# An mLSTM output gate computed with features on the partitions and multiplied in behind the transposition

## The chip, the cores and the metric

The kernel runs on one core of a Trainium2 chip (eight cores on two dies). The metric is the device time of one execution in microseconds (us); lower is better. A core has a matrix engine (TensorE, PE in the profile, PEld its weight loads), a vector engine (VectorE, DVE), a scalar engine (ScalarE, ACT), GpSimd (POOL) and a queue engine (SyncE, SP) that here only issues DMAs. Each engine takes its instructions in the order in which they were built. ScalarE issues DMAs too, in that same order.

## The reference, cut to what matters

One layer of a diffusion backbone over 1024 latent tokens and 256 context tokens, width 1024, in 32-bit floats. Two token mixers, windowed attention and a bidirectional mLSTM, are merged and followed by a ConvFFN. The change is in the end of the mLSTM. With `h_tilde` its output for 4 heads of 256 features:

```python
def mlstm_readout(h_tilde, o_pre, norm_w):
    B, L = h_tilde.shape[:2]
    hn = rms_norm(h_tilde, norm_w.reshape(ML_HEADS, ML_V_DIM)).reshape(B, L, ML_V_W)
    return hn.astype(o_pre.dtype) * jax.nn.sigmoid(o_pre)
```

`o_pre` is a projection of the normed input (1024 tokens x 1024 features to 1024 x 256 per head): the output gate. So each head's output is normed over its 256 features, multiplied by a weight per feature, and by the sigmoid of the gate, element by element. The result then goes through a projection, for which it has to lie with features on the partitions.

## The kernel before, in words

Everything is one program for one core. The stages follow each other: start-up, attention, mLSTM (`stage_mlstm`, L682 to L1086), merge and output projection (`stage_tail`, from L1089), ConvFFN. Every product of two 32-bit matrices is made of three matmuls (`mm3`, L86, lines L91 to L93): each operand is split into a high and a low part (`split_from`, L47: the high part on ScalarE at L44, the low part on VectorE or GpSimd at L49), and high x high, low x high and high x low are added up in PSUM.

The normed input lies transposed in SBUF as `hT`: eight pairs of tiles of 128 features x 1024 tokens. The mLSTM goes through four heads. The loop at L1072 records for each head: `core` (the recurrence over ten chunks in both directions), `decays` of the next head, `proj_o` (the gate), `readout`, then for the next head `proj_kv` and `states`, then `turn` of this head, then `proj_q` and `trans_k` of the next head and three or four `branch_sums`. The order in which the instructions stand on each engine is not that of the recording: a planner of the recording layer sets it, engine by engine, by expected durations and the recorded order as priority, so that matmuls of `proj_o` are laid between those of `core`. What it sets is fixed in the program.

What the steps do, with their lines:

- `core` (L951): `S` = q.k (L961), weighted with the decays on VectorE (`ub`, L965), split into `sh` and `sl`; per chunk and direction two products into PSUM, `o` (L976) and `i` (L978); the numerator `nm` from `i` on ScalarE (L980) and `o` on VectorE (L981); a few short instructions for the denominator (L983 to L985); the output `hf` (L987 on GpSimd or L989 on VectorE). The state: `kwh` on GpSimd (L929), `kwl` on VectorE (L930), the product `dC`, the update `C` on VectorE (L937), and its split into `CH` (ScalarE) and `CL` (VectorE), which the next chunk's `i` reads. `decays` adds masks (`ub`, L910 on GpSimd) and takes exponentials on ScalarE (L912).
- `proj_o` (L766): per head 8 products of 128 tokens x 256 gate features. `hT` is stationary (128 features x 128 tokens), the weights `w1h`, `w1l` move (256 columns): 24 matmuls a product, 192 a head. ScalarE copies each out of PSUM (L774) into `sg`, two tiles for the two halves of 512 tokens; for the last head with the sigmoid.
- `readout` (L1007): the sigmoid over a whole half on ScalarE (L1011, not for the last head), squares and sums of `hf` on ScalarE (`rj`, L1015), the reciprocal root on GpSimd (`rr`, L1016, L1017), and one VectorE instruction per 128 tokens (L1020): `hf` x `rr` x `sg`.
- `turn` (L1022): per half and per 128 features four TensorE transposes (L1028) into a PSUM tile `mt`, one ScalarE copy with the norm weight as scale per partition (L1030) into `mo`, and a store to DRAM on SP (L1031). `mo` has two buffers, shared with the scratch tile of the squares.
- `branch_sums` (L1038): sums and differences of weight and attention tiles for the merge, which have nothing to do with the heads. One round takes both tiles with the tag `sg` (two buffers in all), loads four pieces with DMAs that ScalarE issues (L1046, L1054), makes four VectorE subtractions or additions (L1047 to L1050, L1055 to L1058), and stores four results with DMAs on SP (L1061). Its names are `s_ba`, `t_at`, `s_bm`. Two rounds are recorded within `proj_kv` of the first head, three, four and three behind the `trans_k` of heads 1, 2 and 3.
- `proj_kv` (L723), `proj_q` (L743), `trans_k` (L755): keys, values and queries of a head; the products of `proj_q` have the weights stationary and 512 tokens of `hT` moving, into `q`. PSUM tiles: two for `mm` (kv, q, S, mo), three for `tp` (o, i, transposes).
- In the tail, the first operands of the merge (`baah`, `baal`, `bawh`, `bawl`, products `yb`) are recorded to be issued behind the last instruction of the last readout (`E.turned`, L1020, used at L1228).

The functions that the diff touches and what calls them:

Of the kernel before, what the change touches and what calls it, by code (L numbers as in the profile page):

```python
# [8 lines left out]
F32 = mybir.dt.float32  # L9
F32R = mybir.dt.float32r  # L10
AF = mybir.ActivationFunctionType
ALU = mybir.AluOpType
# [4 lines left out]
P = 128  # L17
# [5 lines left out]
NB = L // P  # L23
# [5 lines left out]
MLH = 4  # L29
DQK = 128  # L30
DV = 256
# [54 lines left out]
def mm3(nc, ps, lhs, rhs, ls, rs, start=True, stop=True):  # L86
    n = len(lhs)
    for i in range(n):
        lh, ll = lhs[i]
        rh, rl = rhs[i]  # L90
        nc.tensor.matmul(ps, lh[:, ls], rh[:, rs], start=start and i == 0, stop=False)  # L91
        nc.tensor.matmul(ps, lh[:, ls], rl[:, rs], start=False, stop=False)  # L92
        nc.tensor.matmul(ps, ll[:, ls], rh[:, rs], start=False, stop=stop and i == n - 1)  # L93


def sl(a, n):
    return slice(a, a + n)
# [3 lines left out]
def layer_kernel(ctx: ExitStack, tc: tile.TileContext, A: dict, out: bass.AP, dbg=None):  # L101
# [76 lines left out]
    with ExitStack() as st:  # L178
        stage_mlstm(E, st)
# [502 lines left out]
def stage_mlstm(E, st):  # L682
    nc, tc, A, ident, expo, hT, wts, dr = E.nc, E.tc, E.A, E.ident, E.expo, E.hT, E.wts, E.dr
    mm_tile, tp_tile, s_tile, mlT_d, gtile = E.mm_tile, E.tp_tile, E.s_tile, E.mlT_d, E.gtile
# [8 lines left out]
    mlw = mp.tile([P, 2 * MLH], F32, name="mlw")  # L693
# [14 lines left out]
    H = {}  # L708
# [46 lines left out]
    def trans_k(h):  # L755
# [7 lines left out]
            kT.append((kh, kl))  # L763
        H[h]["kT"] = kT

    def proj_o(h):  # L766
        w = H[h]["wqo"]
        sgs = [rp.tile([P, 4, DV], F32, tag="sg", name=f"sg{h}_{t}", bufs=2) for t in range(2)]
        for cc in range(NB) if h % 2 else range(NB - 1, -1, -1):
            ps = mm_tile(f"mo{h}_{cc}")  # L770
            mm3(nc, ps[:, :DV], hT, w, sl(cc * P, P), sl(DQK, DV))

            fn = AF.Sigmoid if h == MLH - 1 else AF.Copy
            nc.scalar.activation(sgs[cc // 4][:, cc % 4], ps[:, :DV], fn)  # L774
        H[h]["sg"] = sgs

    GC = {}
# [223 lines left out]
                    seen.add(order[i])  # L1001
        hd["hf"] = hf

    def halves(h):
        return (1, 0) if h % 2 == 0 else (0, 1)

    def readout(h):  # L1007
        hf, sgs = H[h]["hf"], H[h]["sg"]
        for t in halves(h):
            if h < MLH - 1:  # L1010
                nc.scalar.activation(sgs[t], sgs[t], AF.Sigmoid)  # L1011
            rr = rp.tile([P, 8], F32, tag="rr", name=f"rr{h}_{t}", bufs=2)
            for c in range(4):
                junk = rp.tile([P, 512], F32, tag="mo", name=f"rj{h}_{t}_{c}", bufs=2)
                nc.scalar.activation(junk[:, :DV], hf[:, 4 * t + c], AF.Square, accum_out=rr[:, c : c + 1])  # L1015
            nc.gpsimd.tensor_scalar(rr[:, 0:4], rr[:, 0:4], 1.0 / DV, EPS, op0=ALU.mult, op1=ALU.add)  # L1016
            nc.gpsimd.tensor_tensor(rr[:, 4:8], rr[:, 0:4], expo[:, 0:4], op=ALU.pow)  # L1017
            for c in range(4):
                x = hf[:, 4 * t + c]
                E.turned = nc.vector.scalar_tensor_tensor(x, x, rr[:, 4 + c : 5 + c], sgs[t][:, c], op0=ALU.mult, op1=ALU.mult)  # L1020

    def turn(h):  # L1022
        hf = H[h]["hf"]
        for t in halves(h):
            for v in range(2):
                pt = tp_tile(f"mt{h}_{t}_{v}")
                for c in range(4):
                    nc.tensor.transpose(pt[:, c * P : (c + 1) * P], hf[:, 4 * t + c, v * P : (v + 1) * P], ident)  # L1028
                o = rp.tile([P, 512], F32, tag="mo", name=f"mo{h}_{t}_{v}", bufs=2)
                nc.scalar.activation(o, pt, AF.Copy, scale=mlw[:, 2 * h + v : 2 * h + v + 1])  # L1030
                nc.sync.dma_start(mlT_d[h * DV + v * P : h * DV + (v + 1) * P, t * 512 : (t + 1) * 512], o)  # L1031


# [32 lines left out]
    rp = st.enter_context(tc.tile_pool(name="mlr", bufs=2, reuse_waits="tile"))  # L1066
# [5 lines left out]
    for h in range(MLH):  # L1072
        core(h)
        if h + 1 < MLH:
            decays(h + 1)
        proj_o(h)
        readout(h)
        if h + 1 < MLH:
            proj_kv(h + 1)
            states(h + 1)  # L1080
        turn(h)
        if h + 1 < MLH:
            proj_q(h + 1)
            trans_k(h + 1)
            for _ in range((3, 4, 3)[h]):
                branch_sums()  # L1086
# [844 lines left out]
```

## Time and profile before

| what | value |
|---|---|
| median of 3 runs | 1941.0 us (1940.58 to 1943.64) |
| span of the profiled execution (first to last instruction) | 1937.4 us |
| mean granted TensorE clock | 0.999 |
| gate products (mo): matmuls, first to last start | 768, from 712.4 to 1048.2 us |
| copies of the gate out of PSUM (L774): count, median | 32, 0.38 us |
| scaling and gating in the readout (L1020): count, median | 32, 0.48 us |
| copies behind the transposition (L1030): count, median | 16, 0.69 us |
| branch-sum loads, first and last issue | 655.7 and 977.4 us |

The profile is one execution taken by the hardware profiler, separate from the timed runs; what it gives of its own time is the span, and that is 3.6 us below their median (1941.0 - 1937.4). A line of it names the engine, the source line, the operation, the tiles written and read (out<-in, buffer numbers left out), shapes, and the count; behind the bar come total busy time, mean duration, and the idle time just before with what ended it. Matmuls overlap in the array, so the durations of a stream add up to more than the time that it takes. The timeline gives start, duration, and the same names; the view by stages gives for each window the busy time of each engine, the granted clock, and the share and rate of the DMA engines.

### The profile page before, as it was taken

How to read it: one execution, taken by the hardware profiler on the slowest of the kernel's cores; microseconds unless marked ns; L12 is line 12 of the kernel's file. 1: busy time of each engine (PE TensorE's matmuls, PEld its weight loads, DVE VectorE, ACT ScalarE, POOL GpSimd, SP SyncE). 2: the span in 40 equal slices, each digit the busy share in tenths (PEclk: the TensorE clock that was granted, in tenths of full speed). 3: DMA queues.
4: the chain of work that ended last, by engine and by line, in shares of the span. 5: the costliest groups of instructions: out<-in, count | busy, mean ns of one | idle time of the engine just before them, and what ended most of it. 6: DMA issues, size and time to landing. Idle time of an engine off the chain costs nothing.

```text
span 1937.4 us, 28767 instructions
## 1 busy us (share of the span) xinstructions
PE 1903.1 (98%) x10012; PEld 1631.2 (84%) x10012; DVE 1442.4 (74%) x2886; ACT 1000.5 (52%) x1979; POOL 332.0 (17%) x534
## 2 busy tenths in 40 slices
PE   8999999999999999999999999999999999999999
PEld 3998888888888889999999888788888888888887
DVE  2867878777777666666657878669989898897564
ACT  4845656555556445353536556256545444455441
POOL 1323433433333132131311012010000000000000
PEclk9999999999999999999999999999999999999999
DMA  8731222313222323425235982722354534499841
GB/s 320 231 126 51 80 66 67 95 42 102 60 67 77 125 89 104 144 94 192 88 106 210 376 300 89 279 94 77 141 199 182 195 152 177 160 327 341 307 165 65
DMA packets 139377, 298.53 MB, mean 154 GB/s; under 512 B 15440, under 2 KB 39648, under 8 KB 136416
## 3 DMA queue, kind: packets, MB, share of 16 engines
q1 hardware_dynamic: 124832, 270.48, 40.3%
q10 hardware_dynamic: 14400, 26.22, 4.0%
q8 instruction: 78, 1.28, 0.3%
q14 instruction: 67, 0.55, 0.1%
HBM read 220.55 MB, written 76.10 MB: 153 GB/s over the span
## 4 chain that ended last, share of the span: by engine, by line
PE 83%; DVE 5%; DMA 4%; ACT 4%; issue 2%; POOL 1%; POOLq 0%; ACTq 0%; SPq 0%; DVEq 0%
PE pa L1513 4%; PE pa L1515 4%; PE pa L1514 4%; PE pt L625 3%; PE g L93 3%; PE g L92 3%; PE g L91 3%; PE yb L1515 2%; PE yb L1514 2%; PE yb L1513 2%; PE dx L1515 2%; PE dx L1513 2%; PE dx L1514 2%; PE pb L1513 2%; PE pb L1515 2%
## 5 line engine op out<-in xcount | busy, mean ns | idle before, releaser
L606 POOL TENSOR_SCALAR P<-P,st 128x640 f32<-128x640 f32 (+1 forms) x128 | 115.1, 916 | 261.0 <-DVE st L604 178.3
L597 ACT ACTIVATE P<-P,st 128x640 f32<-128x640 f32 (+1 forms) x128 | 102.6, 801 | 24.6 <-DVE st L593 24.0
L593 DVE CUSTOM_DVE_ANT_0 P<-s,maskA,nsink 128x640 f32<-128x640 f32 (+1 forms) x112 | 103.2, 921 | 9.4 <-PE s L590 7.8
L49 DVE TENSOR_TENSOR pl<-pt,ph 128x512 fp32r<-128x512 f32 x152 | 100.8, 686 | 10.1 <-ACT ph L44 8.6
L44 ACT ACTIVATE ph<-pt 128x512 fp32r<-128x512 f32 x152 | 87.4, 597 | 36.9 <-PE pt L625 32.5
L91 PE MATMUL g<-hH,fh 128*128 128x512 f32 x256 | 102.7, 401 | 0.0
L93 PE MATMUL g<-hH,fl 128*128 128x512 f32 x256 | 100.6, 393 | 0.0
L92 PE MATMUL g<-hL,fh 128*128 128x512 f32 x256 | 100.6, 393 | 0.0
L625 PE MATMUL pt<-ident,P 128*128 128x128 f32 x608 | 92.3, 273 | 3.5 <-POOL P L606 3.1
L91 PE MATMUL pq<-w1h,hH 128*128 128x384 f32 (+1 forms) x256 | 87.1, 340 | 0.2 <-DVE t L545 0.2
L91 PE MATMUL kv<-w1h,hH 128*128 128x384 f32 x256 | 86.5, 339 | 0.8 <-ACT w1h L44 0.8
L93 PE MATMUL pq<-w1h,hL 128*128 128x384 f32 (+1 forms) x256 | 86.7, 339 | 0.0
L92 PE MATMUL kv<-w1l,hH 128*128 128x384 f32 x256 | 86.6, 338 | 0.0
L92 PE MATMUL pq<-w1l,hH 128*128 128x384 f32 (+1 forms) x256 | 86.5, 338 | 0.0
L93 PE MATMUL kv<-w1h,hL 128*128 128x384 f32 x256 | 86.3, 337 | 0.0
L625 PEld LDWEIGHTS pt<-ident,P 128*128 128x128 f32 x608 | 71.1, 140 | 11.5 <-POOL P L606 6.4
L91 PE MATMUL mo<-w1h,hH 128*128 128x256 f32 x256 | 72.6, 284 | 0.4 <-ACT sg L774 0.2
L93 PE MATMUL mo<-w1h,hL 128*128 128x256 f32 x256 | 72.1, 282 | 0.0
L92 PE MATMUL mo<-w1l,hH 128*128 128x256 f32 x256 | 71.9, 281 | 0.0
L1651 ACT ACTIVATE cv<-ua,vecT 128x1024 f32<-128x1024 f32 x22 | 27.4, 1245 | 83.6 <-DVE ua L1624 83.6
L929 POOL TENSOR_SCALAR kwh<-k,gcall 128x128 fp32r<-128x128 f32 x72 | 32.7, 457 | 215.8 <-PE dC L92 112.1
L1513 PE MATMUL dx<-dwh,dfh 128*128 128x512 f32 x176 | 68.7, 390 | 0.0
(587 smaller groups left out, 6392.9 us busy)
## 6 DMA issues: line engine op xcount, KB each, us to landing
ur<-in_w_up SPq DMA_DIRECT2D x22, 1024.0 KB, 4.9
wmb<-in_w_modB SPq DMA_DIRECT2D x48, 256.0 KB, 2.9
f_d<-cv SPq DMA_DIRECT2D x22, 512.0 KB, 2.6
wm<-in_w_modA SPq DMA_DIRECT2D x16, 512.0 KB, 9.2
fr<-in_w_g SPq DMA_DIRECT2D x32, 256.0 KB, 3.1
drf<-fs_d SPq DMA_DIRECT2D x15, 512.0 KB, 6.8
drw<-wt_d SPq DMA_DIRECT2D x14, 512.0 KB, 6.0
w1b<-in_w_cx SPq DMA_DIRECT2D x16, 388.0 KB, 4.0
```

Source lines behind the costliest of these rows:

```text
L44: return nc.scalar.activation(out, in_, AF.Copy, scale=scale)
L49: (nc.vector if eng == "v" else nc.gpsimd).tensor_tensor(lo, src, hi.bitcast(F32), op=ALU.subtract)
L91: nc.tensor.matmul(ps, lh[:, ls], rh[:, rs], start=start and i == 0, stop=False)
L92: nc.tensor.matmul(ps, lh[:, ls], rl[:, rs], start=False, stop=False)
L93: nc.tensor.matmul(ps, ll[:, ls], rh[:, rs], start=False, stop=stop and i == n - 1)
L593: nc.vector.tensor_tensor_reduce(pm[:, :W], ps[:, off : off + W], mask[:, :W], scale=ss[:, h : h + 1], scalar=nsink[:, hh : hh + 1], op0=A ...
L597: nc.scalar.activation(pm[:, :W], pm[:, :W], AF.Exp, bias=st4[:, h : h + 1], scale=-1.0, accum_out=st4[:, 4 + h : 5 + h])
L606: nc.gpsimd.tensor_scalar(Ps[h][:, :W], Ps[h][:, :W], st4[:, 12 + h : 13 + h], 1.0, op0=ALU.mult, op1=ALU.mult)
L625: nc.tensor.transpose(pt[:, h * P : (h + 1) * P], Ps[h][:, kb * P : (kb + 1) * P], ident)
L1513: nc.tensor.matmul(ps, lh, rh, start=start and i == 0, stop=False, skip_group_check=True)
L1514: nc.tensor.matmul(ps, lh, rl, start=False, stop=False, skip_group_check=True)
L1515: nc.tensor.matmul(ps, ll, rh, start=False, stop=stop and i == n - 1, skip_group_check=True)
```

## The change

The gate is projected the other way round: the weights are stationary (128 gate features at a time), 512 tokens of `hT` move, so a head has 4 products of 128 features x 512 tokens, 96 matmuls. ScalarE copies each whole PSUM bank into `sg`, whose tiles now hold 2 x 512 instead of 4 x 256 elements a partition. The gate then lies with features on the partitions, as the transposed output does. So the readout only scales with `rr` (a VectorE instruction with one tensor operand), and `turn` multiplies norm weight and gate in one VectorE instruction that reads the transposed tile from PSUM, in the place of ScalarE's copy. `sg` is therefore read in `turn`, no longer in `readout`. `halves` moves up unchanged.

```diff
+    def halves(h):
+        return (1, 0) if h % 2 == 0 else (0, 1)
+
     def proj_o(h):
         w = H[h]["wqo"]
-        sgs = [rp.tile([P, 4, DV], F32, tag="sg", name=f"sg{h}_{t}", bufs=2) for t in range(2)]
-        for cc in range(NB) if h % 2 else range(NB - 1, -1, -1):
-            ps = mm_tile(f"mo{h}_{cc}")
-            mm3(nc, ps[:, :DV], hT, w, sl(cc * P, P), sl(DQK, DV))
-
-            fn = AF.Sigmoid if h == MLH - 1 else AF.Copy
-            nc.scalar.activation(sgs[cc // 4][:, cc % 4], ps[:, :DV], fn)
+        sgs = [rp.tile([P, 2, 512], F32, tag="sg", name=f"sg{h}_{t}", bufs=2) for t in range(2)]
+        for t in halves(h):
+            for v in range(2):
+                ps = mm_tile(f"mo{h}_{t}_{v}")
+                mm3(nc, ps, w, hT, sl(DQK + v * P, P), sl(t * 512, 512))
+
+                fn = AF.Sigmoid if h == MLH - 1 else AF.Copy
+                nc.scalar.activation(sgs[t][:, v], ps, fn)
         H[h]["sg"] = sgs
...
     def readout(h):
...
             for c in range(4):
                 x = hf[:, 4 * t + c]
-                E.turned = nc.vector.scalar_tensor_tensor(x, x, rr[:, 4 + c : 5 + c], sgs[t][:, c], op0=ALU.mult, op1=ALU.mult)
+                E.turned = nc.vector.tensor_scalar(x, x, rr[:, 4 + c : 5 + c], None, op0=ALU.mult)
 
     def turn(h):
-        hf = H[h]["hf"]
+        hf, sgs = H[h]["hf"], H[h]["sg"]
...
                 o = rp.tile([P, 512], F32, tag="mo", name=f"mo{h}_{t}_{v}", bufs=2)
-                nc.scalar.activation(o, pt, AF.Copy, scale=mlw[:, 2 * h + v : 2 * h + v + 1])
+                nc.vector.scalar_tensor_tensor(o, pt, mlw[:, 2 * h + v : 2 * h + v + 1], sgs[t][:, v], op0=ALU.mult, op1=ALU.mult)
                 nc.sync.dma_start(mlT_d[h * DV + v * P : h * DV + (v + 1) * P, t * 512 : (t + 1) * 512], o)
```

More of the change, by code (lines that the diff above doesn't have):

```diff
@@ L1002, in core @@
         hd["hf"] = hf
-    def halves(h):
-        return (1, 0) if h % 2 == 0 else (0, 1)
     def readout(h):
```

## The prediction

> **What bounds the kernel now.** I read the page first, its busy shares and its chain, then the groups of the edited lines, then the stages around them.
>
> ```profile
> span 1937.4 us, 28767 instructions
> PE 1903.1 (98%) x10012; PEld 1631.2 (84%) x10012; DVE 1442.4 (74%) x2886; ACT 1000.5 (52%) x1979; POOL 332.0 (17%) x534
> PE 83%; DVE 5%; DMA 4%; ACT 4%; issue 2%; POOL 1%; POOLq 0%; ACTq 0%; SPq 0%; DVEq 0%
> L91 PE MATMUL g<-hH,fh 128*128 128x512 f32 x256 | 102.7, 401 | 0.0
> L91 PE MATMUL mo<-w1h,hH 128*128 128x256 f32 x256 | 72.6, 284 | 0.4 <-ACT sg L774 0.2
> ```
>
> TensorE (PE) is busy for 98% of the span and carries 83% of the chain that ended last, so what shortens or stalls its stream moves the end. The two groups are products of 512 and of 256 columns. Their mean durations invite a wrong sum: three mo lines of 256 products at 0.28 us are about 217 us, half as many at 0.40 about 154, so 63 us saved. But matmuls overlap, and a stream advances by the distance between starts. The timeline of TensorE has a stretch of nothing but mo, and one of nothing but q, whose operands (weights stationary, hT moving) are those of the new products:
>
> ```profile
> 1037.79 0.28 PE L92 MATMUL mo<-w1l,hH 128*128 128x256 f32 x1
> ...
> 1048.21 0.28 PE L93 MATMUL mo<-w1h,hL 128*128 128x256 f32 x1
> ...
> 699.75 0.40 PE L91 MATMUL q<-hH,w1h 128*128 128x512 f32 x1
> ...
> 707.85 0.40 PE L93 MATMUL q<-hH,w1l 128*128 128x512 f32 x1
> ```
>
> Between the first pair lie 88 starts, so 10.42/88 = 0.1184 us each; between the second 35, so 8.10/35 = 0.2314. The stages come next (columns: window, length, then PE, PEld, DVE, ACT, POOL busy, clock):
>
> ```profile
> 742.00:760.00 18.00, 18.00 (x144) 17.94 (x143) 11.08 (x37) 13.03 (x37) 3.23 (x8) 1.00 0.26 86
> 760.00:792.00 32.00, 31.64 (x182) 30.94 (x181) 15.36 (x26) 7.56 (x20) 0.72 (x2) 1.00 0.62 215
> 806.00:841.00 35.00, 32.65 (x249) 30.43 (x248) 33.03 (x107) 19.49 (x50) 18.59 (x40) 1.00 0.10 31
> 906.00:941.00 35.00, 32.26 (x239) 30.45 (x239) 32.38 (x109) 19.78 (x51) 16.76 (x34) 0.95 0.12 31
> 1005.00:1038.00 33.00, 32.80 (x256) 31.09 (x256) 30.33 (x116) 15.40 (x38) 8.34 (x17) 1.00 0.09 23
> ```
>
> 742 to 760 is the rest of a gate projection behind a core, 760 to 792 a proj_kv; the last three are the cores of heads 1, 2 and 3. In a core VectorE (DVE) is busy 92 to 94% and TensorE idles 2.4 to 2.7 us in heads 1 and 2; in proj_kv VectorE is half idle and TensorE is not held up.
>
> **The change, part by part.** *Products.* 768 at 0.1184 = 90.9 us become 384 at 0.2314 = 88.9: **-2.0 us**, on the path, since TensorE runs these products in any case. The nearest other 512-wide stream (yb, below) gives the other end.
>
> ```profile
> 1054.91 0.39 PE L1515 MATMUL yb<-baah,bawl 128*128 128x512 f32 x1
> 1055.14 0.39 PE L1513 MATMUL yb<-baah,bawh 128*128 128x512 f32 x1
> ```
>
> At its 0.23 the term is -2.6; I keep -2.0, because q has the same operands. [...]
>
> *Evacuations, scaling, transposition.*
>
> ```profile
> L313 DVE TENSOR_SCALAR x<-x,rs x10: 744/753/755, 13.1 to 76.4; 128x1024 f32<-128x1024 f32 x10
> L1020 DVE SCALAR_TENSOR_TENSOR hf<-hf,rr,sg x32: 476/481/486, 750.7 to 1048.9; 128x256 f32<-128x256 f32 x32
> L1030 ACT ACTIVATE mo<-mt,mlw x16: 676/687/696, 792.7 to 1053.6; 128x512 f32<-128x512 f32 x16
> L49 DVE TENSOR_TENSOR pl<-pt,ph 128x512 fp32r<-128x512 f32 x152 | 100.8, 686 | 10.1 <-ACT ph L44 8.6
> ```
>
> ScalarE (ACT) loses the 16 of L1030 (11 us). VectorE gains 16 at about the 0.69 of L49, which also reads PSUM (11 us), and its 32 scalings get cheaper (a quarter of the 0.75 us row to all of 0.48: 0 to -9 us). All of that lies in proj_kv and at the head of the tail, where VectorE has room: nothing on the path. But the output buffers stay two, so the third product of a turn waits for the first store, and that wait moves from ScalarE to VectorE:
>
> ```profile
> 797.98 1.33 ACT L1030 ACTIVATE mo<-mt,mlw 128x512 f32<-128x512 f32 x2 [1.91 <-DMA mlT_d<-mo]
> 796.27 0.95 DVE L49 TENSOR_TENSOR w1l<-w1r,w1h 128x768 fp32r<-128x768 f32 x1
> 794.40 0.26 PE q L91
> mlT_d<-mo SPq DMA_DIRECT2D x16, 256.0 KB, 4.2
> ```
>
> In the built order of the changed kernel, the last split of head 1's query weights (the 796.27 row) stands behind that wait, so it ends at about 799.3 + 1.0 = 800.3, while TensorE wants it at its 21st q product, 794.4 + 20 x 0.2314 = 799.0: **+1.4 us** (0 to 2). In heads 2 and 3 it stands ahead, or the stores are long done; in the tail two operand pieces are split beforehand, 48 products or 11 us of cover for a wait of 4.2. The readout no longer waits for the gate; in head 3 TensorE is anyway filled by mo until 1048.3, so nothing.
>
> *What moves: the branch sums.* Their two buffers are those of sg. Before, the readout freed these; now the turn does, some 40 us later. So the rounds (four loads issued by ScalarE, four subtractions on VectorE, four stores on SP) leave proj_kv and fall into proj_q and the core: three ahead of head 1's gates, four ahead of head 2's, three ahead of head 3's. ScalarE issues the loads in order, and each round waits for the stores of the last.
>
> ```profile
> 867.61 0.83 ACTq L1054 DMA_DIRECT2D t_at<-attT_d  x2
> ...
> 876.20 0.83 ACTq L1054 DMA_DIRECT2D t_at<-attT_d  x2
> ...
> 884.62 0.84 ACTq L1046 DMA_DIRECT2D s_bm<-in_w_bm  x2
> ACT k L44 <- DMA s_ba_d<-s_ba: 4.8, 1, 4.8
> s_ba<-in_w_ba ACTq DMA_DIRECT2D x16, 256.0 KB, 3.9
> s_ba_d<-s_ba SPq DMA_DIRECT2D x16, 256.0 KB, 2.1
> ```
>
> Undisturbed, a round takes 8.4 to 8.6 us from issue to issue (876.20 to 884.62, 867.61 to 876.20). The 4.8 us row is ScalarE's idle time with such an issue ahead of its next evacuation; in proj_kv that costs nothing. In a core, behind the issue stand sh, nm and CH, behind the subtractions sl, nm and CL, and TensorE's o and i products wait for these. Where the core is slower, the round is too: issues 0.8, landing 3.6 to 3.9, three subtractions at 0.6 with as many core instructions between them, store 0.3 + 2.1, about 9.3 us (an estimate). The places where ScalarE is held, at before's times:
>
> ```profile
> 819.13 0.48 ACT L980 ACTIVATE nm<-i,gcall 128x257 f32<-128x257 f32 x1 [0.55 <-PE i L93]
> 895.91 1.40 ACT L1030 ACTIVATE mo<-mt,mlw 128x512 f32<-128x512 f32 x2 [0.70 <-DMA mlT_d<-mo]
> 918.25 0.48 ACT L980 ACTIVATE nm<-i,gcall 128x257 f32<-128x257 f32 x1 [0.65 <-PE i L93]
> 991.65 0.84 ACT L44 ACTIVATE w1h<-w1r 128x768 fp32r<-128x768 f32 x1
> 1014.41 0.48 ACT L980 ACTIVATE nm<-i,gcall 128x257 f32<-128x257 f32 x1 [0.78 <-PE i L93]
> ```
>
> Against the lateness stands a cover: the planner put more gate products ahead of those places. Counted in the built orders at the two spacings (others at 0.12), TensorE has 5.4 us more to do before head 1's place (34 products of 512 for 26 of 256, and others), 4.4 in head 2, 5.8 in head 3.
> - Head 1: buffers free at 797.98 + 1.33 = 799.3; three rounds, 827.2, then one evacuation of 0.6 ahead of nm at 819.1: 8.7 late, 5.4 covered, **3.3**.
> - Head 2: free at 897.3; three rounds, then the issues of the fourth (0.8) ahead of nm at 918.25: 7.8 late, 4.4 covered, **3.4**.
> - Head 3: no store to wait for, first issue 992.5; three rounds and 0.6, ahead of nm at 1014.4: 6.6 late, 5.8 covered, **0.8**.
>
> Together **+7.5**. With rounds of 8.5 it is 1.9; with 10.4 (768.72 to 779.14 in the ScalarE timeline, the longest) 16.3:
>
> ```profile
> 768.72 0.82 ACTq L1046 DMA_DIRECT2D s_ba<-in_w_ba  x2
> ...
> 779.14 0.34 ACTq L1054 DMA_DIRECT2D t_at<-attT_d  x1
> ```
>
> Sum: -2.0 + 1.4 + 7.5 = **+6.9 us** on the profiled span of 1937.4, which gives 1944.3. The page's span is 3.6 us below the runs' median of 1941.0; I carry that over: **1948**.
>
> *Clock.* The row of 906 to 941 has a mean clock of 0.95: 0.05 x 35 = 1.75 us lost in that core. [...]
>
> **The rivals.**
> - *The cover suffices* (28%). Rounds no longer than 8.5 us: -2.0 + 0 to 1.4 + 0 to 1.9, so -2 to +1.3, 1939 to 1942. For it: 8.4 and 8.6 above. Against: these were measured with VectorE half idle.
> - *Faster* (12%). The planner's other order also removes idle time of the cores: up to 2.4 and 2.7 us in heads 1 and 2, with rounds below 8.2 us (799.3 + 3 x 8.2 + 0.6 = 819.1 + 5.4 is where head 1's wait begins to decide). -2.0 - 5.1 = -7.1: 1934. Against: the idle time stands late in the cores, where VectorE is full, and VectorE gets no less to do there.
> - *Weight loads pace the stream* (2%). If 512 columns cost what the load of the weights lasts, 0.188 us, the term is 90.9 - 72.2 = -18.7 and the time 1929. [...] Against: q at 0.2314.
>
> ```profile
> L91 PEld LDWEIGHTS mo<-w1h,hH x256: 186/188/331, 712.4 to 1047.9; 128*128 128x128 f32 x128
> ```
>
> **How the numbers follow.** The forecast (waits beyond the cover) gets 58%: 1943 to 1957. The range leaves out the fastest and slowest ends: 1938 (cover suffices and a little idle time goes) to 1957 (rounds of 10.4: -2.0 + 1.4 + 16.3 = +15.7). A measurement of this kernel can tell about 0.2%, 3.9 us, from no change. Faster by that (below 1937.1): 12 + 2 = 14%. Within: 28%, the second case and no more, since I count the forecast's lower edge against the covered case's upper one. Slower (above 1944.9): 58%.
>
> **What would show it.** Right: TensorE has fewer than 9700 instructions, mo at 0.39 us mean and about 0.23 between starts; branch-sum loads issued within the cores of heads 1 to 3; ScalarE waiting there for s_ba, t_at and s_bm stores, VectorE for their loads; TensorE idle 4 to 6 us in the cores of heads 1 and 2 instead of 2.4 to 2.7, ahead of o and i. Wrong: cores no longer than the added gate products explain (the cover suffices), a time below 1937, or new idle time of TensorE outside the cores, in the tail above all.

## The result, and the profile after

| kernel | median of the runs | runs |
|---|---|---|
| before | 1942.2 us | 1940.6 to 1946.2, 5 runs |
| after | 1964.8 us | 1963.0 to 1971.1, 5 runs |

The ratio is 1.0121 (95% interval 1.0108 to 1.0134): the change makes the kernel 22.6 us slower. The forecast was 1948 us, with a range that ended at 1957. The direction was right, the size a third of what came.

The page of the kernel after (span, busy time by engine, and the chain that ended last by engine):

```profile
span 1969.3 us, 27978 instructions
PE 1915.2 (97%) x9628; PEld 1620.9 (82%) x9628; DVE 1447.5 (74%) x2902; ACT 990.5 (50%) x1947; POOL 333.3 (17%) x534
...
PE 75%; DMA 8%; DVE 8%; ACT 5%; issue 3%; POOL 2%; POOLq 0%; ACTq 0%; SPq 0%; DVEq 0%
```

TensorE has 384 instructions fewer and carries 75% of the chain instead of 83%; DMA rose from 4 to 8%, VectorE from 5 to 8%. The profiled execution is the longest of the five (1971.1 us), 31.9 us of span above that of before; its own parts are read below, and then how they stand to the 22.6 us. By the two pages TensorE's idle time (span less busy time) grew from 34.3 to 54.1 us, which is 19.8 of the 31.9; its busy time grew by the other 12.1, though the new products should take less. 3.6 us of the 31.9 are there before the first product of the mLSTM (654.3 us before, 657.9 after), which the change does not touch.

Where the time lies is seen from the stages. These windows of the kernel after (window, length, then PE, PEld, DVE, ACT, POOL busy, clock) are the cores of heads 1 to 3; the second row is the rest of the gate behind head 1's core:

```profile
809.00:844.00 35.00, 29.44 (x154) 25.36 (x153) 26.60 (x76) 10.60 (x24) 8.45 (x17) 0.80 0.53 181
844.00:862.00 18.00, 16.11 (x84) 13.28 (x83) 16.02 (x55) 11.84 (x32) 11.29 (x25) 0.91 0.01 2
919.00:961.00 42.00, 35.56 (x186) 29.95 (x185) 34.13 (x92) 14.62 (x30) 14.52 (x26) 0.84 0.58 198
1028.00:1063.00 35.00, 32.00 (x192) 27.33 (x191) 31.41 (x103) 13.67 (x32) 8.41 (x19) 0.95 0.30 109
```

Idle time of TensorE in them is 5.6 + 1.9 + 6.4 + 3.0 = 16.9 us. Before, the core windows of heads 1 and 2 had 2.4 and 2.7, the one of head 3 had 0.2. The clock column is as telling: 0.80, 0.91, 0.84 and 0.95 mean up to 7.0 + 1.6 + 6.7 + 1.8 = 17.1 us lost to a halved clock (less where TensorE stood idle at half clock), against 1.75 in one core before. The DMA share of head 1's core went from 0.10 to 0.53: the branch sums are there now.

What TensorE waited for, in the stretches of head 1 (790 to 870), head 2 (890 to 980) and head 3 (985 to 1080): total us, times, longest:

```profile
PE o L91 <- DVE nm L985: 3.2, 1, 3.2
PE S L93 <- DVE kl L49: 1.8, 1, 1.8
...
PE S L91 <- ACT kh L44: 3.5, 1, 3.5
...
PE mo L91 <- DVE ub L969: 2.4, 1, 2.4
```

The S products and their operands `kh` and `kl` are new in this list. Before, no S product waited at all. The chain of waits of the kernel after, in order of time, tells what stands in front of them in head 1 (start, duration, what the end went through):

```profile
799.08 3.27 DMA mlT_d<-mo
802.47 0.76 DVE mo L1031
803.67 5.40 DMA s_ba<-in_w_ba
...
811.26 0.60 DVE ql L49
811.86 0.60 DVE kl L49
813.64 3.69 DMA s_ba<-in_w_ba
...
822.88 7.00 DMA t_at<-attT_d
...
831.68 0.55 PE o L91
```

It reads from top to bottom: the store of a transposed tile holds the last multiplication of `turn`; that one frees the gate's buffer; the first round's load goes into it; the round's subtractions stand on VectorE ahead of `ql` and `kl`, which S needs; the second and third rounds do the same to the core. None of these loads was in the cores before. The ScalarE timeline has the other side, the load issues ahead of `qh` and `kh` in the heads 1 and 2:

```profile
799.08 4.52 ACTq L1047 DMA_DIRECT2D s_ba<-in_w_ba  x3
803.65 0.60 ACT L44 ACTIVATE qh<-q 128x512 fp32r<-128x512 f32 x1 [4.76 <-DVE mo L1031]
...
812.70 0.33 ACTq L1047 DMA_DIRECT2D s_ba<-in_w_ba  x1
...
822.51 1.95 ACTq L1055 DMA_DIRECT2D t_at<-attT_d  x4
...
910.39 4.05 ACTq L1055 DMA_DIRECT2D t_at<-attT_d  x4
...
922.99 0.33 ACTq L1055 DMA_DIRECT2D t_at<-attT_d  x1
923.36 0.60 ACT L44 ACTIVATE kh<-kT 128x512 fp32r<-128x512 f32 x1 [3.81 <-DVE C L941]
...
932.52 0.33 ACTq L1055 DMA_DIRECT2D t_at<-attT_d  x1
```

From issue to issue a round takes 13.6 and 9.8 us in head 1, 12.6 and 9.5 in head 2, and in head 2 the issue at 922.99 is what holds `kh` until 923.36: it stands ahead of `kh` and waits for a store of the round before, issued at 920.87 us (the median landing of these stores is 2.1 us). The row names C, whose end at 923.33 only falls there; in the trace `kh` itself waits for a semaphore of TensorE alone.

Finally the TensorE timeline, with a stall that these rounds make and two gate products at different clocks:

```profile
924.01 0.47 PE L91 MATMUL S<-qh,kh 128*128 128x128 f32 x1 [3.50 <-ACT kh L44]
...
932.27 0.63 PE L91 MATMUL mo<-hH,w1h 128*128 128x512 f32 x1
...
1071.83 0.39 PE L91 MATMUL mo<-hH,w1h 128*128 128x512 f32 x1
```

The same product takes 0.63 us at 932 and 0.39 at 1071: at 932 the granted clock was 0.50 (from 922.6 to 936.2 us), at 1071 it was 1.00.

### The profile page after: what moved, and what is told of

It reads as the page before. It is cut to its first block, busy times and chain, and to the rows that moved or that the text cites. A ratio compares the mean times of both kernels' runs of the same rounds, so it can differ in the third digit from the quotient of the medians.

```text
span 1969.3 us, 27978 instructions
## 1 busy us (share of the span) xinstructions
PE 1915.2 (97%) x9628; PEld 1620.9 (82%) x9628; DVE 1447.5 (74%) x2902; ACT 990.5 (50%) x1947; POOL 333.3 (17%) x534
## 4 chain that ended last, share of the span: by engine, by line
PE 75%; DMA 8%; DVE 8%; ACT 5%; issue 3%; POOL 2%; POOLq 0%; ACTq 0%; SPq 0%; DVEq 0%
PE pa L1514 4%; PE pa L1516 4%; PE pa L1515 4%; PE pt L625 3%; PE g L93 3%; PE g L92 3%; PE g L91 2%; PE dx L1516 2%; PE dx L1514 2%; PE dx L1515 2%; PE pb L1516 2%; PE pb L1514 2%; PE pb L1515 2%; PE po L619 2%; PE kv L91 2%
## 5 line engine op out<-in xcount | busy, mean ns | idle before, releaser
L1516 PE MATMUL dx<-dwh,dfl 128*128 128x512 f32 x176 | 68.6, 390 | 0.0
L1515 PE MATMUL dx<-dwl,dfh 128*128 128x512 f32 x176 | 68.5, 389 | 0.0
L44 ACT ACTIVATE dfh<-drf 128x512 fp32r<-128x512 f32 x55 | 34.4, 628 | 59.0 <-PE dy L1515 25.9
```

Source lines behind the costliest of these rows:

```text
L44: return nc.scalar.activation(out, in_, AF.Copy, scale=scale)
L1515: nc.tensor.matmul(ps, lh, rl, start=False, stop=False, skip_group_check=True)
L1516: nc.tensor.matmul(ps, ll, rh, start=False, stop=stop and i == n - 1, skip_group_check=True)
```

## The experiments

Theory A: the late release of the two buffers that gate and branch sums share makes the loss; the rounds fall into proj_q and the cores and stall TensorE there, and the clock halves (in the kernel after to 0.50 at 830.4 and 922.6 us, in waits of 3.2 and 3.5 us). Rival B: the new VectorE instruction in `turn`, its waits for stores, or the 512-wide products cost by themselves. All medians are in us; the ratio is to runs of the kernel before on the same chip, with its 95% interval.

| kernel | median | before | ratio (interval) | clock in the profile |
|---|---|---|---|---|
| b_late | 1974.9 | 1943.1 | 1.0166 (1.0153 to 1.0180) | 0.993 |
| a_sp | 1958.9 | 1943.1 | 1.0085 (1.0071 to 1.0099) | 0.996 |
| a_turn4 | 1957.0 | 1943.1 | 1.0076 (1.0062 to 1.0089) | 0.994 |
| b_turn4 | 1948.6 | 1943.1 | 1.0029 (1.0017 to 1.0041) | 0.999 |
| b_own | 1957.5 | 1942.0 | 1.0078 (1.0062 to 1.0095) | 0.992 |
| a_own | 1956.2 | 1942.0 | 1.0072 (1.0057 to 1.0087) | 0.994 |
| b_pools | 1945.5 | 1942.2 | 1.0019 (1.0010 to 1.0029) | 0.997 |
| b_own2 | 1950.3 | 1942.2 | 1.0047 (1.0033 to 1.0062) | 0.996 |
| a_own2 | 1944.6 | 1942.2 | 1.0020 (1.0008 to 1.0032) | 0.996 |
| b_core | 1947.7 | 1943.7 | 1.0019 (1.0011 to 1.0028) | 0.997 |
| a_core | 1946.8 | 1943.7 | 1.0020 (1.0011 to 1.0029) | 0.997 |
| a_fin | 1947.5 | 1943.7 | 1.0018 (1.0008 to 1.0028) | 0.995 |
| b_r3 | 1946.7 | 1942.9 | 1.0021 (1.0010 to 1.0031) | 0.997 |
| a_t2 | 1953.9 | 1942.9 | 1.0060 (1.0046 to 1.0075) | 0.997 |
| a_t2i | 1949.7 | 1942.9 | 1.0035 (1.0022 to 1.0049) | 0.997 |

Names with b start from the kernel before, names with a from the kernel after.

### b_late: the late release alone, with the old products

```diff
                 nc.scalar.activation(o, pt, AF.Copy, scale=mlw[:, 2 * h + v : 2 * h + v + 1])
+                if v == 1:
+                    hold = rp.tile([P, 4], F32, tag="hold", name=f"hold{h}_{t}", bufs=2)
+                    nc.vector.tensor_tensor(hold, o[:, 0:4], H[h]["sg"][t][:, 0, 0:4], op=ALU.add)
```

> The kernel before, with the old 256-wide gate products, the gating in the readout and ScalarE's copy behind the transposition. The only addition: behind the second copy of each half, VectorE adds four elements of the gate's buffer to four of the copy (8 instructions of some 0.1 us, into a scratch tile), so that the two buffers which the gate shares with the branch sums come free behind turn and not behind the readout. Theory A (late release: branch-sum rounds fall into proj_q and the cores, hold ScalarE and VectorE there, and stalls of TensorE above 3 us then halve its clock): 1955 to 1968 us, branch-sum loads issued between 797 and 830 us, waits of S for kh or kl, granted clock 0.990 to 0.995. Rival B (the new VectorE instruction in turn, its wait for the stores, or the 512-wide products make the loss): none of them is in here, 1940 to 1945 us, clock 0.999.

Measured: 1974.9 us, 31.8 above before. Nothing of the change is in it but the time at which the buffers come free, and the whole loss is there, and more. The branch-sum loads of head 1 are issued at 794.8 to 818 us, inside proj_q and the core. Waits of TensorE in b_late, 650 to 1260 us (total, times, longest):

```profile
PE o L91 <- ACT sh L44: 6.6, 3, 3.5
PE dC L91 <- DVE C L937: 6.0, 4, 2.9
```

Both are of the core, whose splits and updates stand behind loads and subtractions; the wait of S that the expectation named is nearly absent (0.3 us), and the time is 7 us above the expected range. Rival B is out as the main cause. One reservation: the eight added instructions themselves wait on VectorE for ScalarE's copies, 7.9 us in three waits, so a part of the 31.8 can be theirs. Why b_late is even slower than the kernel after was not tried; the gate products, which fill waits, are cut differently in the two.

### a_sp: the loads issued by SP

```diff
-                nc.scalar.dma_start(o, src)
+                nc.sync.dma_start(o, src)
...
-                nc.scalar.dma_start(o, E.attT_d[r * P : (r + 1) * P, t * 512 : (t + 1) * 512])
+                nc.sync.dma_start(o, E.attT_d[r * P : (r + 1) * P, t * 512 : (t + 1) * 512])
```

> The kernel after, with the branch-sum loads issued by SP instead of ScalarE. ScalarE then has nothing of these rounds in its order. Theory A1 (the hold is mostly ScalarE, whose kh and sh stand behind load issues that wait for buffers): 1943 to 1950 us, no wait of S for kh. Theory A2 (the hold is mostly VectorE, whose kl, ub and sl stand behind subtractions that wait for the loads): 1955 to 1965 us still, S waiting for kl. Rival B (branch sums have no part in it): 1963 to 1968 us.

Measured: 1958.9 us, 15.7 above before instead of 22.6. Taking ScalarE's issues out of its order is worth 6.9 us, three tenths of the loss; the rest stays. TensorE's waits in a_sp, 790 to 1060 us:

```profile
PE o L91 <- ACT sh L44: 5.0, 3, 3.1
PE S L91 <- DVE ql L49: 2.4, 2, 1.4
```

S no longer waits for `kh` on ScalarE but for `ql` on VectorE, and `sh` waits for a `ub` that VectorE makes behind subtractions. So both engines hold the core, VectorE more (A2). SP's own order changed too, which this run doesn't separate.

### a_turn4 and b_turn4: an earlier turn

```diff
+            if h > 0 and j == orders(h)[0][1][4]:
+                turn(h - 1)
+                for _ in range((3, 4, 3)[h - 1]):
+                    branch_sums()
...
-        turn(h)
+        if h == MLH - 1:
+            turn(h)
         if h + 1 < MLH:
             proj_q(h + 1)
             trans_k(h + 1)
-            for _ in range((3, 4, 3)[h]):
-                branch_sums()
```

> The kernel after, with turn of head h and its branch sums recorded within proj_kv of head h + 1, behind the third block of keys and values of the latent tokens, instead of behind proj_kv. In the built order the transposes stand some 45 us earlier in TensorE's stream and all branch-sum loads of heads 1 to 3 stand ahead of ScalarE's qh. Products, gating and turn are those of the kernel after. Theory A: the waits in proj_q and the cores go, clock back at 0.999, and the time is that of the kernel before less the products' 2.0 us: 1936 to 1942 us. Rival B (the VectorE instruction in turn, its store waits or the products): 1955 us or more, since all of these are still in it.

> The kernel before, with turn and branch sums recorded at the same place as in a_turn4. Its buffers come free with the readout in any case, so the earlier turn has nothing to release. Theory A: 1940 to 1944 us, as before, and a_turn4 is 1 to 4 us faster than it (the products' term, -2.0). Rival (the earlier turn by itself is a gain or a loss of its own): outside 1938 to 1946.

Measured: a_turn4 1957.0, b_turn4 1948.6. Theory A missed in both, and a_turn4 lies in the range of rival B, so this pair does not exclude it. b_turn4 shows that the earlier turn has a price of its own, 5.4 us; a_turn4 is 13.9 us above before where the kernel after was 22.6. Its TensorE waits, 790 to 1060 us:

```profile
PE q L93 <- DVE w1l L49: 5.8, 2, 4.2
PE dC L91 <- DVE C L943: 5.5, 4, 1.8
```

Its ScalarE timeline has the first loads of head 1 at 773.8 us and those of the third round at 797.2: 23 us for two rounds. The third is late again, and what stands behind its subtractions is now the split of the query weights. The stall moved with the rounds, from S to q.

### b_own and a_own: buffers of their own

```diff
-    vp = st.enter_context(tc.tile_pool(name="mlv", bufs=13, reuse_waits="tile"))
+    vp = st.enter_context(tc.tile_pool(name="mlv", bufs=10, reuse_waits="tile"))
...
-        two = [rp.tile([P, 4, DV], F32, tag="sg", name=f"{n}{i}_{j}", bufs=2) for j in range(2)]
+        two = [rp.tile([P, 4, DV], F32, tag="bs", name=f"{n}{i}_{j}", bufs=2) for j in range(2)]
...
-    bp = st.enter_context(tc.tile_pool(name="mlb", bufs=15, reuse_waits="tile"))
+    bp = st.enter_context(tc.tile_pool(name="mlb", bufs=14, reuse_waits="tile"))
```

> The kernel before with branch sums in two buffers of their own (tag bs), which are paid for by fewer buffers elsewhere: VH and VL 10 instead of 13, the 512-wide operands of the core 14 instead of 15. The control of a_own. All theories: the branch sums' place in before was not late, so only the price of the smaller pools shows: 1940 to 1950 us.

> The kernel after with the same two buffers for the branch sums and the same smaller pools as b_own; gate, readout and turn as in the kernel after. The release of the gate's buffers no longer concerns the branch sums. Theory A (the late release is the whole loss): 0 to 4 us faster than b_own (the products' -2.0, the store wait's +1.4 at most), clock as in b_own. Rival B (turn on VectorE, its store wait, or the 512-wide products that VectorE and ScalarE's order is planned around cost by themselves): over 8 us slower than b_own.

Measured: 1957.5 and 1956.2. Without the shared buffers the change costs nothing against its control (ratios 1.0072 and 1.0078), as theory A had it. But the control itself is 15.5 us slower than before, which nothing expected. Its ScalarE timeline says why:

```profile
716.46 0.60 ACT L44 ACTIVATE qh<-q 128x512 fp32r<-128x512 f32 x1 [3.39 <-PE q L93]
716.46 4.10 ACTq L1054 DMA_DIRECT2D t_at<-attT_d  x3
720.66 0.63 ACT L44 ACTIVATE sh<-ub 128x512 fp32r<-128x512 f32 x1 [3.61 <-DMA s_ba_d<-s_ba]
```

Nothing holds the rounds back any more, so the planner puts them forward, into proj_q and the core of heads 0 and 1, ahead of `sh`. In the kernel before, the shared buffers had kept them out: they were the schedule.

### b_pools, b_own2 and a_own2: the rounds held behind the readout

b_pools has only the two smaller pools. b_own2 and a_own2 are b_own and a_own with the order below. In the traces it holds the subtractions (in b_own2 from 761.7 us on); the four loads of a head's first round still go out much earlier (683.8 to 685.1), as their buffers are free.

```diff
-            for _ in range((3, 4, 3)[h]):
-                branch_sums()
+            with tc.issue_after(E.turned.ins):
+                for _ in range((3, 4, 3)[h]):
+                    branch_sums()
```

> The kernel before with only the smaller pools of b_own (VH and VL 10 buffers instead of 13, the 512-wide operands 14 instead of 15); the branch sums still share the gate's two buffers. It tells the price of the pools, which was 15 us at most in b_own. Theory A (in b_own the rounds of branch sums, free of the gate's buffers, moved forward into the proj_q and cores of heads 0 and 1, and that cost the 15 us): 1940 to 1946 us. Rival P (the smaller pools cost them): 1952 to 1960 us.

> b_own with the rounds of branch sums issued only behind the last instruction of the readout of the head before (an order, no new work), so that they stand in proj_kv again, as in the kernel before. Theory A: as b_pools, 1940 to 1946 us. Rival P: as b_own, 1952 to 1960 us.

> a_own with the same order: the change as it is in the kernel after, branch sums in buffers of their own and in proj_kv. Theory A (where the rounds stand is the whole loss): 0 to 4 us faster than b_own2, so 1937 to 1944 us, granted clock 0.997 or more, no wait of S or o above 2 us. Rival B (turn on VectorE, its store waits or the products cost by themselves): 1952 us or more. If this is the fastest of all, it is the version that keeps the change and not its cost.

Measured: 1945.5, 1950.3 and 1944.6. The smaller pools cost 3.3 us, not 15: rival P is out. With the rounds back in proj_kv the change is 20 us faster than as it was put in, 2.4 us behind the kernel before and within the price of the pools. a_own2 is just above its expected range, and of the details not all held: one wait of 4.3 us is left, of `dC` for a C that stands on VectorE behind the fourth round of head 2 and the splits that follow it:

```profile
899.54 0.36 PE L91 MATMUL dC<-VH,kwh 128*128 128x258 f32 x1 [4.28 <-DVE C L939]
```

b_own2 is 8.1 us slower than before where 3.3 was due, above its expectation; in its profile `mt` waits 2.5 us for the copy on ScalarE, and the rest was not tracked down. So in this pair the change is 5.7 us faster than its control, more than the products' 2 us, and why is open.

### b_core, a_core and a_fin: released with the core

```diff
-            with tc.issue_after(E.turned.ins):
+            with tc.issue_after(E.cored.ins):
```

where `E.cored` is the last VectorE instruction that writes `hf`. a_fin adds

```diff
-                o = rp.tile([P, 512], F32, tag="mo", name=f"mo{h}_{t}_{v}", bufs=2)
+                o = sgs[t][:, v]
```

with a scratch of 256 columns for the squares, and 11 buffers for VH and VL.

> b_own2 with the rounds of branch sums issued behind the last output of the core of the head before instead of behind its readout: they can begin some 10 us sooner and are over before proj_q. The control of a_core. Theory A (what counts is that no round lies in proj_q or a core): 1942 to 1947 us, the price of the smaller pools (b_pools was +3.3 us) and no more.

> The change with buffers of their own for the branch sums, as in a_own2, with the earlier release of b_core. In a_own2 the fourth round of head 2 still ran into the last block of keys and values (a wait of 4.3 us for C, which stood behind its subtractions). Theory A: that wait goes, 1940 to 1944 us, 0 to 5 us faster than b_core. Rival B (turn on VectorE and its store waits have a price of their own): no faster than a_own2's 1944.6 us and no faster than b_core.

> a_core with turn writing into the gate's buffer in place and storing from it (no mo tile, so VectorE never waits for a store of mlT in turn; the scratch of the squares shrinks to 256 columns) and, for the room that this leaves, VH and VL with 11 buffers instead of 10. Theory A: 1937 to 1943 us, 0 to 3 us faster than a_core; with the pools' price nearly gone it would be at or below the kernel before. If the store waits in turn matter (my prediction gave them 1.4 us), the gain over a_core is above 1 us.

Measured: 1947.7, 1946.8 and 1947.5. The 4.3 us wait is gone, yet a_core stays above its expectation and is no faster than a_own2, which was half of the sign that rival B had named; the other half, a_core against b_core, follows below. b_core and a_fin too are above their ranges. The largest wait of TensorE in a_core, 650 to 1260 us, is now for the weights of proj_kv:

```profile
PE kv L91 <- ACT w1h L44: 5.3, 3, 2.4
```

b_core has the same (4.9 us in 3), so it belongs to this placing of the rounds and not to the change.

a_core against b_core is the cleanest pair (same pools, same release, 12 and 11 runs): 1.0020 and 1.0019. With the rounds placed so, the change by itself is worth 0, with about 2.5 us to either side. The products' 2 us can't be seen in it, and neither can a price of `turn` on VectorE; the two could cancel. In place or not makes nothing here (a_fin).

### b_r3, a_t2 and a_t2i: the old pools, an early turn, three rounds a head

a_t2 is a_turn4 with `orders(h)[0][1][2]` for `[4]` (behind the first block of keys and values, not the third), three rounds a head, and a third round in the first head's proj_kv; b_r3 has only the even rounds; a_t2i writes in place as a_fin does.

> The kernel before with the twelve rounds of branch sums evened out: three a head (a third in the first head's proj_kv, three instead of four behind head 2). Control of a_t2. All theories: rounds lie in proj_kv as before, 1938 to 1944 us.

> The kernel after with its pools and shared buffers, turn and branch sums recorded behind the first block of keys and values (a_turn4: behind the third), and three rounds a head. In the built order the transposes stand two blocks earlier than in a_turn4, where the last round's subtractions stood ahead of the query weights' split and q waited 4.2 us. Theory A: that wait goes, and with it the halved clock: 1937 to 1944 us. If the transposes come so early that they wait for the scaled output, or the last round is late all the same: 1946 to 1955 us, with waits of mt for hf or of q for w1l. Rival B (turn and gating cost by themselves): 1952 us or more.

> a_t2 with turn writing in place into the gate's buffer and storing from there (the third and fourth product of a turn no longer wait for a store of mlT, but the buffers come free only behind the stores). If the store waits delay the release (2.8 us in a_turn4), it is up to 2 us faster than a_t2; if the stores' landing delays it as much, the same within 2 us.

Measured: 1946.7, 1953.9 and 1949.7. Evening out the rounds costs 3.8 us by itself, which its expectation did not have, and a_t2 missed theory A. The large wait of q for `w1l` is gone in a_t2, but the products of proj_kv now wait 9.1 us in nine pieces for `VL`, the split that empties their PSUM tile. VectorE's timeline has it behind a multiplication of `turn` that waits for a store:

```profile
773.99 1.57 DVE L1035 SCALAR_TENSOR_TENSOR mo<-mt,mlw,sg 128x512 f32<-128x512 f32 x2 [5.79 <-DMA mlT_d<-mo]
777.10 0.42 DVE L49 TENSOR_TENSOR VL<-kv,VH 128x256 fp32r<-128x256 f32 x1 [1.54 <-ACT VH L44]
```

In place, without the store waits, that wait of TensorE is 5.6 us in three pieces, and the time is 4.2 us shorter, where at most 2 were expected. So the store waits of `turn`, a part of rival B, do cost where something that TensorE needs stands behind them.

No version with the change came below the kernel before.

## Why the prediction was right or wrong

**Products, -2.0: right.** Two rows of the kernel after, in the stretch that is nothing but gate products in head 3:

```profile
1068.35 0.40 PE L91 MATMUL mo<-hH,w1h 128*128 128x512 f32 x1
...
1076.46 0.39 PE L93 MATMUL mo<-hH,w1l 128*128 128x512 f32 x1
```

35 starts apart, so 8.11/35 = 0.2317 us, against the 0.2314 taken from q; 384 of them are 89.0 us. The rival of weight loads as the pace (0.188) is out.

**Evacuation, scaling, transposition, 0: right** as far as a_core and b_core can tell (1.0020 and 1.0019). The gating takes 0.745 us an instruction (0.69 was taken), the scaling 0.350 instead of 0.48:

```profile
L1031 DVE SCALAR_TENSOR_TENSOR mo<-mt,mlw,sg x16: 739/745/751, 796.5 to 1083.8; 128x512 f32<-128x512 f32 x16
L1021 DVE TENSOR_SCALAR hf<-hf,rr x32: 333/350/385, 754.0 to 1076.1; 128x256 f32<-128x256 f32 x32
```

**The third product's wait for a store, +1.4: the wait came, its price lay elsewhere.** VectorE did wait for the store (802.47 in the chain), but no q product waited for `w1l`. The wait delays the release of the second buffer, and with it the first round: that is its place in the chain above. a_t2i puts 4.2 us on such waits in another order.

**The branch sums, +7.5: the first step that failed.** Mechanism and engines were right: the rounds moved into proj_q and the cores of heads 1 to 3, ScalarE and VectorE wait there, and b_late makes the whole loss out of little else. Three of its sizes were wrong.
- *The round.* 9.3 us was taken; 13.6, 9.8, 12.6 and 9.5 were measured. The first round of a head loads into a buffer that `turn` frees piece by piece, and its subtractions stand in line behind `turn` and `ql`.
- *The place.* I counted the lateness at the end of the rounds, at the `nm` of the core, against a cover of added gate products. The first stalls are before the core: S waits for `kl` (1.8 us) and `kh` (3.5 us), which stand behind the second round's loads and the first's subtractions. In proj_q there are no gate products to lay in front, so there the cover is nothing.
- *The sum over places.* A wait at S does not use up the one at `o` in the same head (1.8 and then 3.2 in head 1), since each later round is late anew.

What the term came to is seen from the first `q` of a head to the first product behind its gates (columns as in the windows above; heads 1, 2 and 3, first before, then after):

```profile
794.20:855.00 60.80, 58.27 (x418) 53.70 (x417) 43.80 (x141) 35.30 (x90) 22.56 (x49) 1.00 0.18 58
892.00:953.80 61.80, 59.04 (x417) 54.80 (x416) 45.96 (x144) 35.33 (x89) 20.47 (x41) 0.97 0.25 80
991.00:1049.60 58.60, 58.38 (x426) 54.20 (x424) 40.74 (x138) 27.22 (x72) 11.81 (x23) 1.00 0.28 100
796.90:868.50 71.60, 64.16 (x322) 53.84 (x321) 51.97 (x151) 31.55 (x80) 21.23 (x46) 0.88 0.39 130
907.10:977.20 70.10, 63.05 (x322) 52.38 (x321) 53.19 (x151) 31.26 (x77) 20.76 (x39) 0.90 0.51 172
1015.60:1077.90 62.30, 59.30 (x329) 49.91 (x328) 48.62 (x152) 26.06 (x66) 11.46 (x25) 0.97 0.47 164
```

The three stretches are 10.8, 8.3 and 3.7 us longer. TensorE idles 4.9, 4.3 and 2.8 us more in them, 12.0 together, where the prediction had 7.5 + 1.4 = 8.9. In the windows of the cores alone it idles 5.6 and 6.4 us in heads 1 and 2, in or close to the 4 to 6 that I had named; with the round and the place wrong, that is luck.

**The clock, 0: the second step that failed, and the larger one in the profiled execution.** The sum has no term for it. TensorE's waits were short (3.2, 3.5, 2.4 and 1.8 us are the longest of the lists above), and the clock halved all the same: it stood at 0.50 for 34.1 us between 813.4 and 1038.6. In the three stretches TensorE is busy 10.8 us longer (175.69 to 186.51), where the products should have made it 1.5 shorter (three quarters of 2.0); so the slower clock cost about 12 us there in the profiled execution, an estimate. How much it takes differs from run to run: the five runs have a mean clock between 0.990 (1971.1 us) and 0.995 (1964.8 us), and 0.005 x 1965 = 9.8 us is more than the 6.4 between them. In the run of the median it is 0.995 against 0.997 in most runs of before (1943 us), some 4 us of the 22.6. So the idle time (19.8 us over the whole profiled execution) is the larger part of the loss, and the clock makes much of the spread.

**The tail.** I named new idle time there as a sign against me. There is some, and the sum had no term for it: the merge's products (yb) take from 1077.9 to 1235.7 us, 157.8, against 153.1 before (1049.6 to 1202.7), with waits for split operands such as this:

```profile
PE yb L1516 <- DVE bmwl L49: 1.6, 1, 1.6
```

In a_core, with the same `turn`, they take 152.6 us (1057.0 to 1209.6), in b_late 153.5 (1082.9 to 1236.4). So it is neither the new turn nor the late rounds alone; what orders these splits late in the kernel after stays open.

**The rivals.** "The cover suffices" and "faster" are both refuted, by the same round lengths. The chance for slower, 58%, was too low given that every displaced round had to find its room on a VectorE that is busy over 90% in the cores; the upper end of the range came from the longest round seen in proj_kv, a stage in which nothing stands in its way. Two of the sums are off, without effect on the outcome: rounds of 10.4 us make 6.6 + 6.7 + 4.1 = 17.4 and not 16.3, which puts the upper end at 1958; and the rival of the weight loads counts the -2.0 twice, so its time is 1931 and not 1929.

## What to carry to other kernels

When an edit moves the last reader of a buffer, list who else takes buffers of that tag, and price the displaced work where it lands: at the first consumer behind it in each engine's order, and at every one after it, not once at the end. A shared tag can be what keeps filler work out of a critical stage; giving the filler buffers of its own cost 15 us, 3 of them for the smaller pools (b_own, b_pools), and an explicit order won back 7 without the change (b_own2) and 12 with it (a_own2). A kernel bound by one engine should have its idle time counted in pieces, as small gaps close together also cost clock here (0.69 and 0.73 us were followed by 3.41 us at 0.50; an estimated 12 us in all in the profiled execution, from pieces of at most 3.5).

## What the runs showed of the hardware that was not expected

In the kernel after, the clock went to half five times between 800 and 1040 us, and no wait of TensorE there is longer than 3.5 us. Ahead of one of the five stand two gaps, 0.69 and 0.73 us, within 3.41 us (the last two rows are these 3.41 us and the 3.41 behind them; behind the length stands PE's busy time, and 1.00 and 0.50 are the clock):

```profile
852.12 0.36 PE L91 MATMUL dC<-VH,kwh 128*128 128x258 f32 x1 [0.69 <-DVE C L941]
...
854.02 0.39 PE L92 MATMUL i<-CL,qh 128*128 128x258 f32 x1 [0.73 <-DVE CL L49]
...
850.91:854.32 3.41, 2.00 (x11) 1.22 (x10) 3.41 (x10) 1.36 (x5) 3.41 (x6) 1.00 0.00 0
854.32:857.73 3.41, 3.41 (x13) 3.02 (x12) 2.65 (x10) 1.87 (x6) 2.30 (x8) 0.50 0.00 0
```

The other four came with a single longer wait. A gap of 2.42 us ended at 1034.8 and one of 1.78 us at 812.5; the half clock began 0.4 and 0.8 us later. In the waits of 3.19 and 3.50 us (ends at 831.7 and 924.0) it began when TensorE had been idle for 1.9 and 2.1 us. By the clock record of this trace the five last 6.83 us from 813.4, 6.83 from 830.4, 3.41 from 854.3, 13.65 from 922.6 and 3.41 from 1035.2; from start to start it is 17.07, 23.89, 68.27 and 112.64 us (5, 7, 20 and 33 times 3.413). In the 3.41 us ahead of each, TensorE was busy 1.63, 1.47, 2.00, 1.32 and 0.99 us. In the cores of the kernel before there is one, 3.41 us from 934.2, with 1.91 us busy ahead of it.

The length of one gap does not tell whether the clock halves: a gap of 1.94 us in the kernel after (to 742.8) and one of 1.87 us in the kernel before (to 737.9) were followed by a clock of 1.00. Nor are the 3 us in the expectation of b_late a limit, as the gaps of 1.78 and 2.42 us show. What decides it, these traces do not show. Why the same kernel loses 0.5 to 1.0% of its clock from run to run was not tested.
